# Neighbourhood attention: normalising the outputs instead of the weights, with value tiles in idle weight buffers

## The chip, the core and the metric

The kernel runs on one core of one Trainium2 chip, as one program. The metric is device time in microseconds: the median of the runs of the kernel before is 2946.88 us (three runs, 2945.25 to 2947.84). PE is the matrix engine, with PEld its weight loads; DVE is VectorE, ACT ScalarE, POOL GpSimd, and SP the engine that only issues DMAs here.

## The reference, cut to what matters

The reference is a transformer block (differential attention beside neighbourhood attention, a mixture of experts, a gated embedding) and two layers of retention and stick-breaking attention. The change lies in the neighbourhood attention: 16 heads of 32 columns over 1024 tokens, seen as a grid of 16 rows and 64 columns. A query looks at 8 rows of keys and, within a block of 32 key columns, at 16 of them; the other columns are masked by the bias.

```python
qb = q_row.reshape(b, ncb, Q_COLS, h, d)            # 4 blocks of 16 query columns
kg = k[:, idx].reshape(b, ncb, kr * K_COLS, h, d)   # 8 rows x 32 columns of keys
vg = v[:, idx].reshape(b, ncb, kr * K_COLS, h, d)
sc = jnp.einsum('bjqhd,bjkhd->bhjqk', qb, kg).astype(jnp.float32) * scale + bias
pr = jax.nn.softmax(sc, axis=-1).astype(vg.dtype)
o = jnp.einsum('bhjqk,bjkhd->bjqhd', pr, vg)
```

The softmax subtracts the row's maximum, exponentiates, and divides by the row's sum. Dividing the weights by the sum before the product with the values, or the product after it, is the same arithmetic.

## The kernel before, in words

The first layer runs `project` (all projections; queries, keys and values go to DRAM), `diff_attention`, `nb_attention` and then the output projection `out_proj`. A planner simulates the program when it is built and orders each engine's instructions by it; each engine then runs its queue strictly in that order, and waits on semaphores. Work of one stage is thus issued inside another where it is ready: loads and splits of a later stage stand in the queues of an earlier one.

`nb_attention` (L453) takes the 16 heads in 4 groups of 4. For a group, the queries of four heads are laid on the diagonal of a block matrix (`qbd`, a high and a low part, L485 on ACT and L486 on POOL), the keys are split into a high and a low part (`kh`, `kl`), and the bias is put together on POOL from DMAs (`edge`, `inner`, L497 and L499). Then come four column blocks (`cb`). In each, eight row pairs of queries give eight tiles of 128 rows (4 heads x 2 grid rows x 16 columns) by 256 or 288 keys:

- three matmuls on PE into a bank `sc` (L522 to L524);
- bias and row maximum in one DVE instruction into `P` (L531);
- in two batches of four tiles: the maxima negated on DVE (L534), four exponentials on ACT that also give the row sums (L536), the reciprocal of four sums on DVE (L538), four normalisations on POOL (L540), four transposes on DVE into `pt` (L542), which turn 32x32 blocks.

When all eight tiles are transposed, 16 fp32 matmuls (L551), one per grid row of keys, add the value products of the whole column block into one bank `po`; the first covers all eight tiles, so it needs all transposes. The values of four heads lie on the diagonal of `vbd`, zeroed once by POOL (`zero`, L439) and loaded by four DMAs on SP per block (L508). There are two such tiles, taken in turn. Four copies, two on ACT and two on DVE (L558, L556), bring `po` to `cat`. `P` has eight buffers, `sc` six banks, `po` two.

The weights of `project` and `out_proj` come in chunks of 256 columns: a raw tile `wraw` (one buffer, `w_raw`, L125) is split by ACT and DVE into `whi` and `wlo` (two buffers each, L113 and L114). `out_proj` (L564) takes chunk 0 for tiles 0 to 3, chunk 1 for tiles 0 to 3, and then tiles 4 to 7 of both. In `diff_attention` the q tiles are loaded by POOL's own DMA queue (L377); `lv` and `lp` are small tiles from which lambda is computed.

Of the kernel before, what the change touches and what calls it, by code (L numbers as in the profile page):

```python
# [7 lines left out]
F32 = mybir.dt.float32  # L8
F32R = mybir.dt.float32r
I32 = mybir.dt.int32  # L10
AF = mybir.ActivationFunctionType
OP = mybir.AluOpType
# [32 lines left out]
class Kernel:  # L45
# [289 lines left out]
    def diff_attention(self, cat):  # L335
        tc, nc, I = self.tc, self.nc, self.I
        lam_init = 0.8 - 0.6 * math.exp(0.0)
        with self.banks(mm=2, tp=2, sp=2), self.pool(name="a2k", bufs=2, side="right") as kp, \
                self.pool(name="a2", bufs=2) as wp, self.pool(name="a2c", bufs=1) as cp:

            lv = cp.tile([128, 4, 64], F32, name="lv")
            for j, n in enumerate(("lam_q1", "lam_k1", "lam_q2", "lam_k2")):
                nc.sync.dma_start(lv[:, j], dap(I[n], 0, [[0, 128], [1, 64]]))
            lp = cp.tile([128, 2, 64], F32, name="lp")
            nc.vector.tensor_mul(lp, lv[:, 0:4:2], lv[:, 1:4:2])
# [24 lines left out]
            for h in range(4):  # L370
# [4 lines left out]
                for qt in range(NT):  # L375
                    qr = kp.tile([128, 2, 2, 128], F32R, name="q", bufs=3)
                    nc.gpsimd.dma_start(qr.rearrange("p m c t -> p (m c t)"), self.q_d[h, qt])  # L377
                    sm = self.small.tile([128, 2], F32, name="dsm")
                    e = []
                    for m in range(2):  # L380
                        s = self.s_ps()
# [15 lines left out]
                    for hf in range(2):  # L397
                        p = self.t_ps()
# [42 lines left out]
    def nb_consts(self, cp):  # L441


        qbd = [[cp.tile([128, 2, 8, 4, 32], F32R, name="qbd%s%d" % (n, hf)) for n in "hl"] for hf in range(2)]
        vbd = [cp.tile([128, 16, 128], F32, name="vbd%d" % j) for j in range(2)]
        for hl in qbd:
            for t in hl:
                self.zero(t.rearrange("p c r h q -> p (c r h q)"), 2048)
        for t in vbd:
            self.zero(t.rearrange("p r d -> p (r d)"), 2048)  # L450
        return qbd, vbd

    def nb_attention(self, ep, cat, qbd, vbd):  # L453
# [6 lines left out]
        with self.banks(sc=6, po=2), self.pool(name="a3", bufs=2) as wp, self.pool(name="a3c", bufs=1) as cp:  # L460
# [4 lines left out]
            for j in range(2):  # L465
                t = cp.tile([128, 3744], F32, name="pt%d" % j)
                for row in (6 * NR + 1, 6 * NR + 13):
                    nc.vector.memset(t[:, row * 32:row * 32 + 32], 0.0)
                pt.append(t)
            rmk = cp.tile([128, 9, 32], F32, name="rmk")  # L470
            nc.sync.dma_start(rmk, I["c_nbmask"][:, 96:].rearrange("p (r k) -> p r k", r=9))
            for g in range(4):
# [31 lines left out]
                for cb in range(4):  # L504
                    vb, pT = vbd[cb % 2], pt[cb % 2]
                    for h in range(4):
# [3 lines left out]
                    qh, ql = (t[:, cb % 2].rearrange("p r h q -> p r (h q)") for t in qbd[cb // 2])  # L510
                    for rp0 in (0, 4):
                        mx = self.small.tile([128, 4], F32, name="nmx")
                        sm = self.small.tile([128, 4], F32, name="nsm")
                        ps4 = []
                        for j in range(4):
                            rp = rp0 + j
# [7 lines left out]
                            nc.tensor.matmul(ps[:, :n], ql[:, rp], khv[kv], start=False, stop=True)  # L524
                            p = wp.tile([128, 288], F32, name="P", bufs=8)[:, :n]
                            if nr == 9:
                                bv = inner[KIND[cb]]
                            else:
# [3 lines left out]
                                                           op1=OP.max, scale=1.0, scalar=-3e38, accum_out=mx[:, j:j + 1])  # L532
                            ps4.append((p, rp, r0, n))
                        nc.vector.tensor_scalar(mx, mx, -1.0, None, op0=OP.mult)  # L534
                        for j, (p, rp, r0, n) in enumerate(ps4):
                            nc.scalar.activation(p, p, AF.Exp, bias=mx[:, j:j + 1], accum_out=sm[:, j:j + 1])  # L536
                        rc = self.small.tile([128, 4], F32, name="nrc")
                        nc.vector.reciprocal(rc, sm)  # L538
                        for j, (p, rp, r0, n) in enumerate(ps4):
                            nc.gpsimd.tensor_scalar(p, p, rc[:, j:j + 1], 1.0, op0=OP.mult, op1=OP.mult)  # L540
                            o = (rp * NR + r0 - 2 * rp + 6) * 32
                            nc.vector.transpose(pT[:, o:o + n], p)  # L542


                    po = self.bank("po")
                    for kr_ in (7, *range(7), *range(8, 16)):
                        have = [rp for rp in range(8) if kr_ == 7 or first(rp * 2) <= kr_ < first(rp * 2 + 1) + 8]
                        a, m = have[0], len(have)
                        o = (a * NR + kr_ - 2 * a + 6) * 32
                        w = pT[:, o:o + m * (NR - 2) * 32].rearrange("p (m x) -> p m x", m=m)[:, :, :32]  # L550
                        nc.tensor.matmul(po[:, a * 32:(a + m) * 32], vb[:, kr_], w, start=kr_ == 7, stop=kr_ == 15)  # L551
                    for j in range(4):
                        o = cat[j][:, 4 + g].rearrange("p (r c) -> p r c", c=64)[:, :, cb * 16:cb * 16 + 16]
                        s = po[:, j * 64:j * 64 + 64].rearrange("p (r q) -> p r q", q=16)
                        if j % 2:
                            nc.vector.tensor_copy(o, s)  # L556
                        else:
                            nc.scalar.activation(o, s, AF.Copy)  # L558

# [987 lines left out]
```

## Time and profile before

| what | value |
| --- | --- |
| median of the runs | 2946.88 us |
| profiled execution, its own time | 2949.21 us |
| its span | 2947.4 us |
| mean granted clock of PE | 0.967 |
| busy share of the span: PE, DVE, ACT, POOL | 92%, 72%, 60%, 24% |
| DMA | 512.92 MB, mean 174 GB/s |

The busy shares are means over the whole span; the neighbourhood attention is only the stretch from about 541 to 711 us of it. In the rows below, a timeline row gives the start, the duration, the engine, the line, the operation with output and inputs, the count of merged instructions, and in brackets the idle time before it with what ended it. The granted clock is 1.00 at 2.4 GHz and 0.50 at 1.2 GHz; a value between is a mean over a stretch.

### The profile page before, as it was taken

The page shows a single profiled execution, that of the slowest core. Times are in us where ns is not written, and L with a number is a line of the kernel's source. Part 1 is how long each engine was busy: PE and PEld are TensorE (multiplying, and loading weights), DVE is VectorE, ACT ScalarE, POOL GpSimd, SP SyncE. Part 2 cuts the span into 40 slices and gives each one's busy share as a digit, 9 for nine tenths or more (in the row PEclk, how much of TensorE's full clock was granted, in tenths as well). Part 3 has the DMA queues.
Part 4 walks back from the last instruction along what each step waited for, and adds up shares of the span by engine and source line. Part 5 has one row for each costly group of instructions (what it writes and reads, how often), then busy time and mean ns, then how long its engine had stood idle before and what let it go on. Part 6 is the DMA issues. An engine that isn't in the chain of part 4 may idle for free. (4 is left out here: it accounts for less than half of the span.)

```text
span 2947.4 us, 49384 instructions
## 1 busy us (share of the span) xinstructions
PE 2710.2 (92%) x17751; PEld 2447.2 (83%) x17751; DVE 2127.2 (72%) x4362; ACT 1760.7 (60%) x3827; POOL 718.0 (24%) x847
## 2 busy tenths in 40 slices
PE   7999889788979999999959799999989899999988
PEld 7998878678968777877749788999889788899888
DVE  6778589676389888999965458899355368898354
ACT  4444467554258878888846357788342367788242
POOL 0343131563001102111024101650123102650132
PEclk9999999889989999999979899999999899999999
DMA  7766432324279989999851333322562342331661
GB/s 237 248 204 204 130 79 69 64 50 141 109 272 328 314 313 355 368 363 367 308 211 70 115 120 96 98 87 75 199 217 73 116 128 88 98 95 65 223 190 72
DMA packets 390010, 512.92 MB, mean 174 GB/s; under 512 B 94948, under 2 KB 236284, under 8 KB 389252
## 3 DMA queue, kind: packets, MB, share of 16 engines
q1 hardware_dynamic: 375364, 480.37, 49.3%
q0 software_dynamic: 14400, 29.38, 3.0%
q8 instruction: 141, 2.31, 0.3%
q14 instruction: 105, 0.86, 0.1%
HBM read 425.71 MB, written 101.97 MB: 179 GB/s over the span
## 5 line engine op out<-in xcount | busy, mean ns | idle before, releaser
L150 PE MATMUL mm<-whi,acth 128*128 128x256 f32 x2816 | 812.0, 288 | 20.5 <-ACT acth L113 5.7
L152 PE MATMUL mm<-whi,actl 128*128 128x256 f32 x2816 | 807.4, 287 | 6.4 <-DVE rsx L100 3.8
L151 PE MATMUL mm<-wlo,acth 128*128 128x256 f32 x2816 | 804.8, 286 | 0.0
L150 PEld LDWEIGHTS mm<-whi,acth 128*128 128x128 f32 x2816 | 543.7, 193 | 31.7 <-ACT acth L113 7.9
L152 PEld LDWEIGHTS mm<-whi,actl 128*128 128x128 f32 x2816 | 542.6, 193 | 11.0 <-DVE rsx L100 4.3
L151 PEld LDWEIGHTS mm<-wlo,acth 128*128 128x128 f32 x2816 | 543.2, 193 | 3.0 <-issue 0.9
L114 DVE TENSOR_TENSOR wlo<-mraw,whi 128x512 fp32r<-128x512 f32 x508 | 316.1, 682 | 46.7 <-ACT whi L113 46.4
L113 ACT ACTIVATE whi<-mraw 128x512 fp32r<-128x512 f32 x508 | 276.1, 628 | 11.5 <-PE mm L879 9.3
L114 DVE TENSOR_TENSOR wlo<-wraw,whi 128x2048 fp32r<-128x2048 f32 (+1 forms) x64 | 145.5, 2278 | 138.9 <-ACT whi L113 129.1
L1198 PE MATMUL mm<-acth,whi 128*128 128x512 f32 x512 | 201.7, 394 | 0.0
L1200 PE MATMUL mm<-acth,wlo 128*128 128x512 f32 x512 | 201.1, 393 | 0.0
L1199 PE MATMUL mm<-actl,whi 128*128 128x512 f32 x512 | 200.5, 392 | 0.0
L113 ACT ACTIVATE whi<-wraw 128x2048 fp32r<-128x2048 f32 (+1 forms) x64 | 117.0, 1833 | 102.0 <-PE mm L152 67.6
L1240 POOL TENSOR_TENSOR cN<-rx,rcos 128x256 f32<-128x256 f32 x64 | 63.4, 990 | 444.2 <-ACT rx L1237 440.4
L114 DVE TENSOR_TENSOR mlo<-mraw,mhi 128x512 fp32r<-128x512 f32 x256 | 160.2, 680 | 2.9 <-ACT mhi L113 1.6
L1373 ACT ACTIVATE sw<-sw 128x128 f32<-128x128 f32 (+2 forms) x192 | 100.8, 528 | 70.5 <-DVE sw L1372 69.5
L113 ACT ACTIVATE mhi<-mraw 128x512 fp32r<-128x512 f32 x256 | 140.6, 631 | 2.9 <-PE mm L879 2.9
L920 POOL DMA_INDIRECT y_d<-ey,sidx x32 | 39.0, 1219 | 373.5 <-ACT ey L919 364.8
L1366 DVE SCALAR_TENSOR_TENSOR sw<-z,sw 128x128 f32<-128x128 f32 (+1 forms) x192 | 103.8, 547 | 30.3 <-ACT sw L1365 29.5
L1386 DVE TENSOR_TENSOR sal<-tp,sah 128x512 fp32r<-128x512 f32 (+1 forms) x192 | 101.8, 546 | 25.4 <-ACT sah L1385 24.8
L1363 ACT ACTIVATE sw<-z 128x128 f32<-128x128 f32 (+1 forms) x192 | 93.3, 491 | 38.2 <-DVE z L1360 38.0
L1200 PEld LDWEIGHTS mm<-acth,wlo 128*128 128x128 f32 x512 | 96.2, 188 | 19.6
(361 smaller groups left out, 6776.0 us busy)
## 6 DMA issues: line engine op xcount, KB each, us to landing
mraw<-in_w_dram SPq DMA_DIRECT2D x191, 1024.0 KB, 9.0
wraw<-in_w_in_dram SPq DMA_DIRECT2D x88, 512.0 KB, 4.8
mw<-in_w_ada_dram SPq DMA_DIRECT2D x32, 768.0 KB, 6.7
wraw<-in_w_out_dram SPq DMA_DIRECT2D x24, 512.0 KB, 5.3
q_d<-qo SPq DMA_DIRECT2D x32, 256.0 KB, 3.2
q<-q_d POOLq DMA_DIRECT2D x32, 256.0 KB, 2.9
h_d<-res SPq DMA_DIRECT2D x16, 512.0 KB, 2.7
sqk<-sq_d SPq DMA_DIRECT2D x32, 256.0 KB, 4.1
```

The source lines that it names most:

```text
L113: nc.scalar.activation(hi, raw, AF.Copy)
L114: nc.vector.tensor_sub(lo, raw, hi.bitcast(F32))
L150: nc.tensor.matmul(ps[:, :n], ah[:, k, sl], wh[:, k, :n], start=k == 0, stop=False)
L151: nc.tensor.matmul(ps[:, :n], ah[:, k, sl], wl[:, k, :n], start=False, stop=False)
L152: nc.tensor.matmul(ps[:, :n], al[:, k, sl], wh[:, k, :n], start=False, stop=k == kt - 1)
L1198: nc.tensor.matmul(ps, wh[:, k, cs], hh[:, k], start=k == 0, stop=False)
L1199: nc.tensor.matmul(ps, wh[:, k, cs], hl[:, k], start=False, stop=False)
L1200: nc.tensor.matmul(ps, wl[:, k, cs], hh[:, k], start=False, stop=k == 7)
L1363: nc.scalar.activation(a, z, AF.Abs)
L1366: nc.vector.scalar_tensor_tensor(a, z, 0.0, a, op0=OP.max, op1=OP.add)
L1373: nc.scalar.activation(a, a, AF.Exp)
L1386: nc.vector.tensor_sub(al[ts], pv, ah[ts].bitcast(F32))
```

## The change

Four value tiles replace two: the third and fourth are one buffer of `whi` and one of `wlo`, used as fp32 while the weights don't need them; all four are zeroed by POOL, and column block `cb` always uses tile `cb`. To make room, `lv` and `lp` live in the raw weight buffer. Tiles go in pairs instead of batches of four; the maxima are negated on ACT; the exponentials are transposed as they are. The eight sums of a column block get one reciprocal; POOL spreads it along a diagonal (`dg`, 128x256), one matmul with a 0/1 matrix (`hd1`) brings every reciprocal to all 32 partitions of its head in the second half of the `po` bank, ACT copies it out (`rb`), and DVE multiplies the outputs by it on their way to `cat`. `P` has six buffers.

```diff
-            lv = cp.tile([128, 4, 64], F32, name="lv")
+            lb = self.w_raw()
+            lv = lb[:, 0:256].rearrange("p (j d) -> p j d", j=4)
...
         vbd = [cp.tile([128, 16, 128], F32, name="vbd%d" % j) for j in range(2)]
+        vbd += [self.W.tile([128, 2048], F32, name="vbd", tag=t, bufs=2).rearrange("p (r d) -> p r d", d=128)
+                for t in ("whi", "wlo")]
...
+            hd1 = cp.tile([128, 4, 32], F32, name="hd1")
+            eye = cp.tile([128, 32], F32, name="eye")
+            nc.vector.memset(hd1, 0.0)
+            for h in range(4):
+                b = slice(h * 32, h * 32 + 32)
+                nc.vector.memset(hd1[b, h], 1.0)
+                nc.scalar.activation(eye[b], self.ident[b, b], AF.Copy)
...
-                    vb, pT = vbd[cb % 2], pt[cb % 2]
+                    vb, pT = vbd[cb], pt[cb % 2]
...
-                    for rp0 in (0, 4):
+                    sm = self.small.tile([128, 8], F32, name="nsm")
+                    for rp0 in range(0, 8, 2):
...
-                            p = wp.tile([128, 288], F32, name="P", bufs=8)[:, :n]
+                            p = wp.tile([128, 288], F32, name="P", bufs=6)[:, :n]
...
-                        nc.vector.tensor_scalar(mx, mx, -1.0, None, op0=OP.mult)
-                        for j, (p, rp, r0, n) in enumerate(ps4):
-                            nc.scalar.activation(p, p, AF.Exp, bias=mx[:, j:j + 1], accum_out=sm[:, j:j + 1])
-                        rc = self.small.tile([128, 4], F32, name="nrc")
-                        nc.vector.reciprocal(rc, sm)
-                        for j, (p, rp, r0, n) in enumerate(ps4):
-                            nc.gpsimd.tensor_scalar(p, p, rc[:, j:j + 1], 1.0, op0=OP.mult, op1=OP.mult)
+                        nc.scalar.activation(mx, mx, AF.Copy, scale=-1.0)
+                        for j, (p, rp, r0, n) in enumerate(ps2):
+                            nc.scalar.activation(p, p, AF.Exp, bias=mx[:, j:j + 1], accum_out=sm[:, rp:rp + 1])
                             o = (rp * NR + r0 - 2 * rp + 6) * 32
                             nc.vector.transpose(pT[:, o:o + n], p)
+                    rc = self.small.tile([128, 8], F32, name="nrc")
+                    nc.vector.reciprocal(rc, sm)
+                    dg = wp.tile([128, 8, 32], F32, name="dg", bufs=1)
+                    nc.gpsimd.tensor_tensor(dg, eye.unsqueeze(1).to_broadcast([128, 8, 32]),
+                                            rc.unsqueeze(2).to_broadcast([128, 8, 32]), op=OP.mult)
...
+                    nc.tensor.matmul(po[:, 256:512], hd1.rearrange("p h q -> p (h q)"), dg.rearrange("p r q -> p (r q)"),
+                                     start=True, stop=True)
+                    rb = wp.tile([128, 256], F32, name="rb", bufs=1)
+                    nc.scalar.activation(rb, po[:, 256:512], AF.Copy)
                     for j in range(4):
                         o = cat[j][:, 4 + g].rearrange("p (r c) -> p r c", c=64)[:, :, cb * 16:cb * 16 + 16]
-                        s = po[:, j * 64:j * 64 + 64].rearrange("p (r q) -> p r q", q=16)
-                        if j % 2:
-                            nc.vector.tensor_copy(o, s)
-                        else:
-                            nc.scalar.activation(o, s, AF.Copy)
+                        nc.vector.tensor_mul(o, po[:, j * 64:j * 64 + 64].rearrange("p (r q) -> p r q", q=16),
+                                             rb[:, j * 64:j * 64 + 64].rearrange("p (r q) -> p r q", q=16))
```

## Rows read from the trace of the kernel before

**Rows 1.** Windows: start:end, length, busy us (instructions) by engine, clock, DMA.
```profile
541.00:712.00 171.00, 138.35 (x923) 132.98 (x924) 125.52 (x492) 95.14 (x321) 117.41 (x176) 0.89 0.35 66
...
541.00:584.00 43.00, 34.66 (x212) 32.83 (x213) 32.38 (x115) 22.96 (x73) 36.78 (x50) 0.84 0.46 78
...
627.00:669.00 42.00, 33.96 (x228) 32.70 (x229) 31.78 (x134) 23.25 (x81) 30.96 (x47) 0.88 0.21 39
669.00:711.00 42.00, 35.27 (x255) 34.28 (x254) 31.00 (x126) 22.49 (x80) 18.58 (x38) 0.96 0.33 72
```

**Rows 2.** Timeline of PE, starts of chains of value products.
```profile
555.13 2.46 PE L551 MATMUL po<-pt,vbd 128*128 128x256 f32 x16 [0.87 <-DVE pt L542]
...
591.53 4.31 PE L551 MATMUL po<-pt,vbd 128*128 128x256 f32 x16 [4.60 <-issue]
...
600.75 4.29 PE L551 MATMUL po<-pt,vbd 128*128 128x256 f32 x32
...
681.58 2.36 PE L551 MATMUL po<-pt,vbd 128*128 128x256 f32 x16
...
688.86 1.37 PE L551 MATMUL po<-pt,vbd 128*128 128x256 f32 x9
...
702.16 4.36 PE L551 MATMUL po<-pt,vbd 128*128 128x256 f32 x32 [2.39 <-issue]
```

**Rows 3.** Timeline of POOL around 590 us.
```profile
582.46 6.18 POOL L486 TENSOR_TENSOR qbdl<-qT,qbdh 32x512 fp32r<-32x512 f32 x4
...
589.82 3.78 POOL L540 TENSOR_SCALAR P<-P,nrc 128x288 f32<-128x288 f32 x8
```

**Rows 4.** Groups by line, 541 to 712: count | busy, mean ns | idle before, releasers.
```profile
L536 ACT ACTIVATE P<-P,nmx 128x256 f32<-128x256 f32 (+1 forms) x128 | 65.1, 510 | 56.1 <-DVE nmx L534 55.2 <-DVE cat L556 0.8
L540 POOL TENSOR_SCALAR P<-P,nrc 128x256 f32<-128x256 f32 (+1 forms) x128 | 61.7, 503 | 35.9 <-DVE nrc L538 29.2 <-DVE nmx L534 6.3
L542 DVE STREAM_TRANSPOSE pt<-P 128x256 f32<-128x256 f32 (+1 forms) x128 | 56.4, 451 | 12.4 <-POOL P L540 12.2
...
L486 POOL TENSOR_TENSOR qbdl<-qT,qbdh 32x512 fp32r<-32x512 f32 x24 | 31.4, 1307 | 5.4 <-ACT qbdh L485 4.0
...
L531 DVE CUSTOM_DVE_ANT_0 P<-sc,inner 128x288 f32<-128x288 f32 x64 | 26.8, 432 | 2.6 <-PE sc L524 2.3
...
L534 DVE TENSOR_SCALAR nmx<-nmx 128x4 f32<-128x4 f32 x32 | 12.9, 404 | 0.3
...
L499 POOL TENSOR_TENSOR inner<-edge,rmk 128x288 f32<-128x288 f32 x12 | 9.6, 805 | 0.3
L556 DVE COPY cat<-po 128x64 f32<-128x64 f32 x32 | 7.0, 217 | 8.9 <-ACT cat L558 8.9
...
L538 DVE RECIPROCAL nrc<-nsm 128x4 f32<-128x4 f32 x32 | 5.3, 167 | 16.7 <-ACT P L536 16.5
```

**Rows 5.** Timeline of ACT, two small operations of the projection.
```profile
352.21 0.21 ACT L102 ACTIVATE rsy<-rsx 128x8 f32<-128x8 f32 x1
...
356.27 0.47 ACT L330 ACTIVATE bo<-tp,gbk 128x256 f32<-128x256 f32 x1 [3.61 <-PE tp L321]
```

**Rows 6.** Line 534, durations min/median/max in ns.
```profile
L534 DVE TENSOR_SCALAR nmx<-nmx x32: 127/170/2710, 546.5 to 697.8; 128x4 f32<-128x4 f32 x32
```

**Rows 7.** Timeline of SP, reload of a value tile.
```profile
679.78 1.55 SPq L508 DMA_DIRECT2D vbd<-vb_d  x3
```

**Rows 8.** Timelines of DVE and PE, weight split and output projection.
```profile
352.00 2.29 DVE L114 TENSOR_TENSOR wlo<-wraw,whi 128x2048 fp32r<-128x2048 f32 x1 [1.17 <-ACT whi L113]
...
710.32 6.89 DVE L114 TENSOR_TENSOR actl<-cat,acth 128x1024 fp32r<-128x1024 f32 x6
...
721.18 0.39 PE L150 MATMUL mm<-whi,acth 128*128 128x256 f32 x1 [0.70 <-DVE res L601]
```

**Rows 9.** Timelines of POOL and PE, zeroing and the fourth q load.
```profile
367.06 5.05 POOL L439 TENSOR_SCALAR vbd<-one 128x1024 f32<-128x1024 f32 x4
...
375.98 2.09 PE L385 MATMUL sp<-ks,q 128*128 128x512 f32 x8 [0.53 <-DMA q<-q_d]
```

More of the change, by code (lines that the diff above doesn't have):

```diff
@@ L339, in diff_attention @@
                 self.pool(name="a2", bufs=2) as wp, self.pool(name="a2c", bufs=1) as cp:
-            lv = cp.tile([128, 4, 64], F32, name="lv")
+            lb = self.w_raw()
+            lv = lb[:, 0:256].rearrange("p (j d) -> p j d", j=4)
             for j, n in enumerate(("lam_q1", "lam_k1", "lam_q2", "lam_k2")):
                 nc.sync.dma_start(lv[:, j], dap(I[n], 0, [[0, 128], [1, 64]]))
-            lp = cp.tile([128, 2, 64], F32, name="lp")
+            lp = lb[:, 256:384].rearrange("p (j d) -> p j d", j=2)
             nc.vector.tensor_mul(lp, lv[:, 0:4:2], lv[:, 1:4:2])
@@ L510, in nb_attention @@
                     qh, ql = (t[:, cb % 2].rearrange("p r h q -> p r (h q)") for t in qbd[cb // 2])
-                    for rp0 in (0, 4):
[L512 to L515, printed above, removed]
+                    sm = self.small.tile([128, 8], F32, name="nsm")
+                    for rp0 in range(0, 8, 2):
+                        mx = self.small.tile([128, 2], F32, name="nmx")
+                        ps2 = []
+                        for j in range(2):
                             rp = rp0 + j
@@ L532, in nb_attention @@
                                                            op1=OP.max, scale=1.0, scalar=-3e38, accum_out=mx[:, j:j + 1])
-                            ps4.append((p, rp, r0, n))
-                        nc.vector.tensor_scalar(mx, mx, -1.0, None, op0=OP.mult)
-                        for j, (p, rp, r0, n) in enumerate(ps4):
-                            nc.scalar.activation(p, p, AF.Exp, bias=mx[:, j:j + 1], accum_out=sm[:, j:j + 1])
-                        rc = self.small.tile([128, 4], F32, name="nrc")
-                        nc.vector.reciprocal(rc, sm)
-                        for j, (p, rp, r0, n) in enumerate(ps4):
-                            nc.gpsimd.tensor_scalar(p, p, rc[:, j:j + 1], 1.0, op0=OP.mult, op1=OP.mult)
+                            ps2.append((p, rp, r0, n))
+                        nc.scalar.activation(mx, mx, AF.Copy, scale=-1.0)
+                        for j, (p, rp, r0, n) in enumerate(ps2):
+                            nc.scalar.activation(p, p, AF.Exp, bias=mx[:, j:j + 1], accum_out=sm[:, rp:rp + 1])
                             o = (rp * NR + r0 - 2 * rp + 6) * 32
                             nc.vector.transpose(pT[:, o:o + n], p)
+                    rc = self.small.tile([128, 8], F32, name="nrc")
[3 more added lines that the diff above has]
+                                            rc.unsqueeze(2).to_broadcast([128, 8, 32]), op=OP.mult)
                     po = self.bank("po")
```

## The prediction

> **What bounds the kernel now.** I first looked at the windows of the stretch in which the changed lines run, 541 to 711 us: in 171 us PE is busy 138, DVE 126, POOL 117, ACT 95, and PE's granted clock is 0.84 in the first group, 0.88 in the third, 0.96 in the last [rows 1]. No engine is full. The stage is 16 column blocks (4 groups x 4 values of cb), each ending in one chain of value products, po. So I read PE's timeline for the starts of po: first 555.13, the thirteenth (group 3 begins) 681.58, last 702.16 [rows 2]. Twelve intervals take 126.45 us, 10.54 each; the last three 20.58, 6.86 each. The same work per block at two paces: that difference is what to explain.
>
> In the fast part PE is the limit: between 681.58 and 688.86 (7.28 us) it waits for nothing. In the slow part po is seen to wait, 4.60 us before 591.53 [rows 2]. POOL's timeline says why: it runs the low parts of the next group (L486) for 6.18 us from 582.46, and only from 589.82 the eight normalisations (L540, 3.78 us) whose results the transposes of this block need [rows 3]. POOL's load per block of groups 0 to 2: L540 is 61.7 / 16 = 3.9 us, L486 and L499 are (31.4 + 9.6) / 13 = 3.2 (what is left of them after 541 lies in about the first 13 blocks) [rows 4]. Work due now queues behind work due a group later. The groups by line show who waits in turn: ACT 55.2 us for the negated maximum, POOL 29.2 for the reciprocal, DVE 12.2 for POOL and 8.9 for ACT's copy out of the same bank [rows 4]. Exponential, reciprocal, normalisation, transpose is a round trip over ACT, DVE, POOL and DVE in batches of four.
>
> **The change part by part.**
>
> *Normalising moves from the weights to the outputs.* 128 L540 leave POOL (61.7 us) and the round trip. Added per block: one product 128x256 on POOL (dg; nearest row L499, 128x288, 0.8 us), one fp32 product on PE, one ACT copy 128x256 out of PSUM (rb; nearest row L330, 0.47 us [rows 5]), four DVE products 128x64 in place of two DVE and two ACT copies; one reciprocal of the two goes. The PE product: po's 32 records (16 matmuls, each recorded twice) go over 2240 columns by the loop's bounds and take 4.36 us [rows 2], so 256 columns take 4.36 x 256 / 2240 = 0.50. A DVE product reads PSUM and writes cat like the copy L556, 217 ns [rows 4]: 0.9 a block for 0.44 today. dg can start when the last exponential is done, while the last transposes and 4.36 us of po still run; that hides the reciprocal, dg and most of what may stand ahead of it on POOL. Without that cover PE stands on the product (a rival below).
>
> *Negation on ACT, pairs for fours.* 32 negations leave DVE (12.9 us), 64 smaller ones come to ACT at 0.21 (L102, 128x8 [rows 5]): 13.4 us. A negation takes 127 ns at least, 170 in the median and 2710 at most [rows 6]: on DVE it sometimes stands still. The Trainium skill (SBUF — State Buffer, "Who interferes with whom") has a rule that would do this: a VectorE instruction in a two-port mode and a GpSimd instruction shut each other out for a whole instruction. By it, 12.9 - 32 x 0.17 = 7.5 us of DVE's stage vanish beyond the work itself; if the long ones are only waits for the maxima, nothing does. The sum needs neither, since DVE is not what limits it. ACT after: 95 + 13.4 + 16 x 0.47 = 116 us, 7.2 a block. P has six buffers for eight, but a pair's way (two reductions 0.9, negation 0.2, two exponentials 1.0, two transposes 0.9 [rows 4, 5]) is 3.0 us, and three pairs at once pass four of them in 4.0 us: fewer buffers don't bind.
>
> *Four value buffers.* A reload waits for the po of two blocks before. But that of block 13 is issued from 679.78 on and done issuing at 681.3, over seven us ahead of its po at 688.86, and no wait of that po is seen [rows 2, 7]. I cost this part at 0; loads queued on SP behind it are for a group ahead. Bounds: from a gain of 2 us to a loss of 1.
>
> *What the weight buffers give up.* Today w_out's first two chunks are split before the stage. Now one whi and one wlo hold values until the last po, so chunk 0 takes chunk 1's place at 352 and chunk 1 is split after the stage. It is due when chunk 0's first four tiles are through, at 721.18 today, where PE waits 0.70 us for the residual anyway; DVE's splits of cat run from 710.32 for 6.89 us, and even behind all of them a split of 2.29 ends at 719.5 [rows 8]. Cost 0 to 2 us; I take 0.5. lam's rows pass through the raw buffer ahead of chunk 0, whose split waits till 352 in any case: 0. Zeroing two more buffers repeats today's row of four instructions, 5.05 us. If it stands ahead of the q load that POOL issues at 372, PE, which today waits 0.53 us for that load, waits up to 5 more; if it runs in POOL's idle time before, 0 [rows 9]. I take 2.
>
> **The new pace.** PE's floor is 7.28 + 0.50 = 7.78. DVE: 125.5 - 12.9 (negations) - 2.6 (half of the reciprocals) - 7.0 (copies) + 64 x 0.22 = 117, 7.3 a block. POOL: 117.4 - 61.7 + 16 x 0.8 = 69. PE comes first, with DVE and ACT close behind, in queues that run in order. The interval 591.53 to 600.75, 9.22 us, ends without a wait of po [rows 2]: a block of the first groups with POOL not in the way and the rest uneven. I take the middle of 7.78 and 9.22, 8.5.
>
> **Sum**, against the profiled execution's 2949.2 us: twelve intervals 12 x (8.5 - 10.54) = -24.5; three at the end +0.5 each, +1.5; the first po earlier, as two trips over POOL go, -3 (0 to -5); behind the last po the product, rb and one DVE product, +1.0, ahead of it a reciprocal and a normalisation less, -1.0; zeroing +2; w_out +0.5. Together -23.5, 2925.7; the median of the runs is 2.3 below the profiled one, so 2923.4.
>
> **Rivals.**
> - *PE at its floor* (0.12). Twelve intervals at 7.78, -33; first po -5; +1.5: 2910. For it: at the end PE goes without a gap already. By the rows the clock is higher where PE waits least (0.96 in the last group). The Trainium skill (TensorE: Matmul & The Clock Gate, "What's actually happening") says that a monitor sets the clock by how busy the array has lately been; by that rule closing the gaps gives the clock back as well, and this case follows. Against: DVE at 7.3 and ACT at 7.2 leave little slack.
> - *The trip still sets the pace* (0.16). ACT's 55.2 us on the maxima are DVE against ACT, without POOL. If only POOL's lumps go, intervals fall from 10.54 to 9.7, -10; with 0 to +4 of the other terms 2937 to 2941, and 2944 if the first po gains nothing.
> - *Slower: the product becomes a gate* (0.12). PE runs in order. If the product stands straight behind po and dg waits on POOL behind the next group's L486 (6.18 us at a stretch), PE stops; rb on ACT then stops the exponentials behind it, and the products on DVE the transposes behind them. A full stop costs reciprocal 0.17, dg 0.8, product 0.5, rb 0.47, DVE 0.9: 2.8 a block, 45 us over 16, so -23.5 + 45: 2968. It decides from 23.5 / 16 = 1.5 us a block on, that is when dg ends 1.5 us after po. Against it: POOL has 49 us less to do, and the next block's scores can stand in between.
> - My forecast, a gain of 12 to 32 us: 0.60 (2914 to 2935 on the runs' scale).
>
> **Range and chances.** 0.2% (5.9 us) is about what a measurement of this kernel can tell from no change. Faster: forecast, floor and half of the third case, 0.80; the same: the other half and mild gates, 0.10; slower: 0.10. For 8 in 10, 2908 to 2941.
>
> **What would show it.** Right: po's starts 8 to 9 us apart in groups 0 to 2; nothing of POOL between exponential and transpose; granted clock over 0.9; POOL near 69 us; the residual still what PE meets first at the output projection. Wrong: PE or ACT waiting for dg or rb over 1 us a block; exponentials still 50 us on maxima; over 4 us on a q load near 376; PE waiting for chunk 1's wlo.

## The result and the profile after

The changed kernel takes 2915.34 us in the median of four runs (2912.77 to 2921.78), against 2946.07 for the kernel before on the same chip: ratio 0.9898, 95% interval 0.9882 to 0.9914. That is faster, and inside the predicted range. The predicted 2923.4 was 8 us too high, and the pace came out as the first rival had it (7.75 us an interval, where it had 7.78). The execution that was profiled took 2921.78, 6.4 above its median; the account below is made against it and the 2949.21 of before.

The windows of the stage, from its first score to the output projection's first product; columns as in [rows 1]:

```profile
539.65:672.20 132.55, 126.66 (x929) 123.72 (x929) 112.70 (x473) 105.22 (x366) 65.50 (x64) 0.98 0.36 64
539.65:583.00 43.35, 42.64 (x300) 41.92 (x301) 39.70 (x162) 36.43 (x124) 30.04 (x30) 0.93 0.56 100
583.00:628.00 45.00, 43.72 (x331) 42.94 (x330) 38.82 (x168) 38.05 (x138) 27.29 (x26) 1.00 0.42 76
```

PE is now busy for 126.66 of 132.55 us, 96%, where it was 138.35 of 171, 81% [rows 1]. Its busy time fell although new products came to it; the granted clock rose from 0.89 to 0.98.

The same view of the twelve intervals alone, before and after:

```profile
555.13:681.58 126.45, 101.94 (x673) 97.92 (x674) 92.17 (x365) 70.95 (x246) 95.06 (x139) 0.88 0.32 56
548.51:641.49 92.98, 91.00 (x686) 89.29 (x685) 81.77 (x350) 79.11 (x274) 58.64 (x56) 1.00 0.46 82
```

PE's idle time there falls from 24.5 us to 2.0, and its busy time by 10.9, at a granted clock of 1.00 in place of 0.88: of the 33.5 us that went, two thirds are waits of PE and one third is busy time, which got shorter at the higher clock although new products came to it.

PE's timeline, starts of po (first, eighth, thirteenth and last of the sixteen):

```profile
548.51 2.36 PE L566 MATMUL po<-pt,vbd 128*128 128x256 f32 x16
...
604.68 2.46 PE L566 MATMUL po<-pt,vbd 128*128 128x256 f32 x16 [1.28 <-DVE pt L550]
...
641.49 2.35 PE L566 MATMUL po<-pt,vbd 128*128 128x256 f32 x16
...
663.14 2.45 PE L566 MATMUL po<-pt,vbd 128*128 128x256 f32 x16
```

Twelve intervals take 641.49 - 548.51 = 92.98 us, 7.75 each, against 10.54 in [rows 2]; the last three 7.22 each, against 6.86. Of sixteen chains only that at 604.68 shows a wait ahead of its start. In the mean the two paces of before have become nearly one; single intervals still range from 6.3 to 9.9 us.

The groups by line in the stage (count | busy, mean ns of one | idle before, releasers):

```profile
L548 ACT ACTIVATE P<-P,nmx 128x256 f32<-128x256 f32 (+1 forms) x128 | 65.6, 513 | 1.5
L550 DVE STREAM_TRANSPOSE pt<-P 128x256 f32<-128x256 f32 (+1 forms) x128 | 54.1, 443 | 8.3 <-ACT P L548 7.7
L498 POOL TENSOR_TENSOR qbdl<-qT,qbdh 32x512 fp32r<-32x512 f32 x24 | 32.3, 1347 | 7.2 <-ACT qbdh L497 5.8
L546 ACT ACTIVATE nmx<-nmx 128x2 f32<-128x2 f32 x64 | 12.3, 196 | 14.3 <-DVE nmx L543 13.9
L567 PE MATMUL po<-dg,hd 128*128 128x256 f32 x32 | 10.2, 402 | 0.0
L556 POOL TENSOR_TENSOR dg<-eye,nrc 128x256 f32<-128x256 f32 x16 | 9.9, 617 | 40.2 <-DVE nrc L554 40.2
L573 DVE TENSOR_TENSOR cat<-po,rb 128x64 f32<-128x64 f32 x64 | 9.7, 212 | 0.0
L570 ACT ACTIVATE rb<-po 128x256 f32<-128x256 f32 x16 | 5.9, 371 | 8.8 <-PE po L567 8.6
```

ACT's wait for the maxima, 56.1 us ahead of the exponentials in [rows 4], is now 1.5 there and 14.3 ahead of the negations. The added operations cost nearly what the nearest rows gave: POOL's product 0.62 (estimated 0.8), rb 0.37 (0.47), the products of the outputs 0.21 (0.22). The product on PE cost less than the 0.50 that was estimated. Its two records overlap with their neighbours, so the step from start to start counts, 553.67 - 553.37 = 0.30 us in the first block, and 0.24 to 0.30 in 14 of the 16:

```profile
553.37 0.65 PE L567 MATMUL po<-dg,hd 128*128 128x256 f32 x2
553.67 0.48 PE L534 MATMUL sc<-kh,qbdh 128*128 128x288 f32 x1
```

PE never waits for dg (0.0 ahead of L567): POOL itself stood idle 40.2 us until the reciprocals came.

The lumps are still on POOL's queue, but nothing of the trip passes them. POOL's timeline:

```profile
582.29 0.62 POOL L556 TENSOR_TENSOR dg<-eye,nrc 128x256 f32<-128x256 f32 x1
582.86 3.96 POOL L498 TENSOR_TENSOR qbdl<-qT,qbdh 32x512 fp32r<-32x512 f32 x3
...
590.23 0.62 POOL L556 TENSOR_TENSOR dg<-eye,nrc 128x256 f32<-128x256 f32 x1
```

**Where the 27.4 us of the two profiled executions come from.** Each line is the difference between starts that both traces show; the last one reaches to the time of the execution:

| stretch | before | after | difference |
| --- | --- | --- | --- |
| to the first score | 541.1 | 539.6 | -1.4 |
| first score to first po | 14.1 | 8.9 | -5.2 |
| twelve intervals | 126.45 | 92.98 | -33.5 |
| last three intervals | 20.6 | 21.7 | +1.1 |
| last po to the experts' first transpose | 150.1 | 155.9 | +5.7 |
| the experts | 626.9 | 624.1 | -2.8 |
| last expert product to the next layer's first transposed product (L1198 before), the gated embedding between them | 197.6 | 204.3 | +6.7 |
| all behind it | 1272.4 | 1274.4 | +2.0 |

Up to the last po 39.0 us were gained, 37.6 of them in the stage, more than I said; 5.7 went right behind it, and the 2100 us from the experts on, which the change doesn't touch, lost 5.9 more.

**The 5.7 us behind the last po.** Timelines of DVE, SP and PE after:

```profile
668.51 2.29 DVE L114 TENSOR_TENSOR wlo<-wraw,whi 128x2048 fp32r<-128x2048 f32 x1 [1.72 <-PE po L566]
...
670.90 0.48 DVE L573 TENSOR_TENSOR cat<-po,rb 128x64 f32<-128x64 f32 x3
...
687.49 1.42 DVE L617 TENSOR_TENSOR res<-mm,res 128x256 f32<-128x256 f32 x4 [6.16 <-DMA res<-in_x_dram]
```
```profile
670.87 0.95 SPq L122 DMA_DIRECT2D wraw<-in_w_out_dram  x2
672.12 0.37 SPq L609 DMA_DIRECT2D res<-in_x_dram  x1
```
```profile
672.18 0.58 PE L150 MATMUL mm<-whi,acth 128*128 128x256 f32 x1 [3.22 <-ACT acth L113]
```

The split of the second weight chunk stands on DVE ahead of the last products with rb, of which the first starts at 670.77 and the row shows the other three; PE waits 3.22 us for the output projection, against 1.40 before. The same split frees the raw weight buffer, so the load of the third chunk now stands on SP at 670.87 right ahead of the residual's. In the kernel before the third chunk came at 354 and the residual was issued 4.4 us after the last po began, not 9.0:

```profile
354.32 0.94 SPq L122 DMA_DIRECT2D wraw<-in_w_out_dram  x2
...
706.55 0.38 SPq L593 DMA_DIRECT2D res<-in_x_dram  x1
```

The first sum with the residual comes 15.3 us behind the first product of the projection (687.49 - 672.18), against 720.7 - 707.9 = 12.8.

**Zeroing.** POOL's timeline has the two tiles that it now zeroes before the q loads in one stretch of idle time, and PE's timeline the q load that [rows 9] has:

```profile
326.16 4.10 POOL L440 TENSOR_SCALAR vbd<-one 128x1024 f32<-128x1024 f32 x4 [39.96 <-PE mm L151]
```
```profile
377.87 2.12 PE L386 MATMUL sp<-ks,q 128*128 128x512 f32 x8 [0.42 <-DMA q<-q_d]
```

The wait is 0.42 us, against 0.53 before.

### The profile page after: what moved, and what is told of

The parts are those of the page before. It is cut to its first block, busy times and chain, and to the rows that moved or that the text cites. A ratio compares the mean times of both kernels' runs of the same rounds, so it can differ in the third digit from the quotient of the medians.

```text
span 2919.7 us, 49355 instructions
## 1 busy us (share of the span) xinstructions
PE 2709.7 (93%) x17783; PEld 2449.4 (84%) x17783; DVE 2118.4 (73%) x4351; ACT 1772.3 (61%) x3879; POOL 669.0 (23%) x739
## 4 chain that ended last, share of the span: by engine, by line
PE 51%; DVE 18%; issue 12%; DMA 8%; ACT 8%; POOL 2%; SPq 1%; DVEq 0%; ACTq 0%; POOLq 0%
PE mm L152 6%; PE mm L150 6%; PE mm L151 6%; PE mm L1214 3%; PE mm L1215 3%; PE mm L1216 3%; DVE sw L1383 3%; PE mm L893 3%; PE mm L895 3%; PE mm L894 3%; PE po L566 2%; DVE wlo L114 2%; DMA sqk<-sk_d 2%; PE mm L406 2%; PE sp L386 2%
```

## The experiments

Every kernel was timed beside the kernel before on its own chip, so ratios are compared. The stretches are those of the one profiled execution of each kernel, which lies up to 6.4 us from its median. "Interval" is (start of the thirteenth po minus start of the first) / 12; "stage" reaches from the first score to the start of the last record of po (165.1 us before, 128.6 after); "end" from there to the experts' first transpose; "embedding" from the last expert product to the first transposed product (L1198 before) of the layer behind the gated embedding; the gated embedding itself lies within that stretch.

| kernel | ratio to before, 95% | interval | stage | end | embedding |
| --- | --- | --- | --- | --- | --- |
| before | 1 | 10.54 | 165.1 | 146.1 | 197.6 |
| after | 0.9898, 0.9882 to 0.9914 | 7.75 | 128.6 | 150.8 | 204.3 |
| e1_two_values | 0.9889, 0.9874 to 0.9903 | 7.88 | 129.2 | 146.4 | 202.9 |
| e2_four_values_only | 1.0005, 0.9995 to 1.0016 | 10.57 | 167.2 | 145.9 | 204.5 |
| e7_no_low_parts | 0.9953, 0.9937 to 0.9969 | 8.82 | 144.5 | 145.3 | 201.8 |
| e5_pool_pairs | 0.9982, 0.9973 to 0.9992 | 10.16 | 158.4 | 145.9 | 200.7 |
| e10_pool_load2 | 0.9937, 0.9923 to 0.9952 | 8.65 | 141.3 | 154.5 | 191.9 |
| e6_fours | 0.9924, 0.9906 to 0.9942 | 9.21 | 143.9 | 147.7 | 201.6 |
| e3_neg_on_dve | 0.9885, 0.9866 to 0.9904 | 8.21 | 134.1 | 150.9 | 192.1 |
| e4_neg_on_act_only | 0.9959, 0.9944 to 0.9973 | 9.68 | 153.9 | 146.7 | 200.7 |
| e11_neg_by_reduce | 0.9993, 0.9982 to 1.0004 | 10.25 | 161.7 | 146.4 | 198.6 |
| e12_pairs_neg_by_reduce | 0.9869, 0.9849 to 0.9889 | 8.00 | 131.0 | 150.4 | 195.0 |
| e8_turn_rb | 0.9847, 0.9828 to 0.9865 | 7.69 | 125.8 | 148.1 | 192.9 |
| e9_turn_rb_two_values | 0.9878, 0.9861 to 0.9895 | 7.87 | 127.4 | 146.7 | 196.6 |

### What are four value tiles worth? (e1_two_values, e2_four_values_only)

e1 is the kernel after with two value tiles, and lam's rows in their own tiles again; e2 makes the opposite edit in the kernel before. Of e1's edit:

```diff
-        vbd += [self.W.tile([128, 2048], F32, name="vbd", tag=t, bufs=2).rearrange("p (r d) -> p r d", d=128)
-                for t in ("whi", "wlo")]
...
-                    vb, pT = vbd[cb], pt[cb % 2]
+                    vb, pT = vbd[cb % 2], pt[cb % 2]
```

> The changed kernel with two value tiles again, both weight buffers left to w_out, and lam's rows in their own tile. Theory (the gain is the normalisation leaving POOL and the round trip; the reload of a value tile is never what po waits for): the first twelve intervals between po's starts stay at 7.7 to 7.9 us, the time stays within 3 us of the changed kernel, perhaps 1 to 2 us shorter because chunk 1 of w_out is split before the stage again: 2912 to 2918. Rival (SP's 59 us of waiting for po were part of the slow pace, so four tiles carry a part of the gain): intervals of 8.3 or more, 2924 or more.

> The kernel before with the four value tiles alone. Theory: nothing is gained, intervals stay near 10.5, 2943 to 2949 (0 to +3 for the later split of chunk 1). Rival: a gain of 8 us or more, 2938 or less.

e1 took 2915.7 us and e2 2951.1: neither differs from its base by what can be measured. Four tiles bring nothing in either kernel. In the kernel after they also cost: with the weight buffers left alone, the end is 146.4 us in place of 150.8, so of the 5.7 us the 4.7 that the end lost go with the buffers that are lent out (the rest lies in the last po itself). Lending alone doesn't cost this: e2 and e5 lend the same buffers, their split stands behind the last po too, and their end is 145.9. There a first copy of po runs on ACT beside the split, and the residual's load is issued ahead of the third chunk's (707.07 and 709.43 in e2). So the rows put the price on the lending together with outputs that are all multiplied on DVE behind the split, and with the order on SP; the shares of these two were not separated. In e1's total the saving doesn't show beyond the scatter.

### Lumps on POOL's queue, or the trip itself? (e7_no_low_parts, e5_pool_pairs, e10_pool_load2)

e7 is the kernel before without the low parts of the queries in groups 1 to 3, so these groups use the low parts of group 0. e5 is the kernel after with the weights normalised on POOL again, in pairs. e10 is e1 with POOL's load put back, but as products that only need the row sum and whose output nobody uses. (The first form, e10_pool_load, gave this output a tile of its own; the pool then needs 32.5 kb a partition where 31.9 are left, so there is no time for it.)

```diff
# e7
-                        nc.gpsimd.tensor_tensor(lo, s, hi.bitcast(F32), op=OP.subtract)
+                        if g == 0:
+                            nc.gpsimd.tensor_tensor(lo, s, hi.bitcast(F32), op=OP.subtract)
# e5 (and no dg, product, rb; outputs copied as before)
+                        rc = self.small.tile([128, 2], F32, name="nrc")
+                        nc.vector.reciprocal(rc, sm[:, rp0:rp0 + 2])
+                        for j, (p, rp, r0, n) in enumerate(ps2):
+                            nc.gpsimd.tensor_scalar(p, p, rc[:, j:j + 1], 1.0, op0=OP.mult, op1=OP.mult)
# e10
                             nc.vector.transpose(pT[:, o:o + n], p)
+                            nc.gpsimd.tensor_scalar(scr[:, :n], rmk.rearrange("p r k -> p (r k)")[:, :n],
+                                                    sm[:, rp:rp + 1], 1.0, op0=OP.mult, op1=OP.mult)
```

> The kernel before without the low parts of the queries in groups 1 to 3 (the instructions of POOL that make them are left out, so those scores use group 0's low parts): POOL loses 31 us of lumps up to 6.2 us, the normalisation stays on POOL. Theory (work due a group later stands in POOL's queue ahead of work due now): the first twelve intervals fall from 10.5 to 8.5 or less, 2920 to 2930. Rival (the round trip over four engines itself sets the pace, lumps or not): intervals of 9.8 or more, 2938 or more.

> The changed kernel with the weights normalised on POOL again, in pairs, with the copies of po as before; four value tiles, pairs and the negation on ACT stay. Theory (normalising on a POOL queue that is also filled with the next group's work is what slowed it): intervals of 9.5 to 10.5, PE seen waiting for transposes and DVE for POOL, 2935 to 2948. Rival (batches of four and DVE's negation made the round trip long, pairs shorten it, POOL may stay in it): intervals of 8.5 or less, 2925 or less.

> The kernel after with two value tiles (as e1_two_values, 2915.7), and POOL given 128 extra products of 128x256 or 128x288, at the places where the kernel before normalised the weights, with an operand that is ready only after the exponential; their output is used by nobody. So POOL's load is as before the change, but nobody waits for these products except dg, which stands behind them in POOL's queue. Theory (about 21 of the 33 us came from the lumps on POOL's queue, the rest from the trip by itself): intervals 8.2 to 9.2, as dg is late behind the lumps, 2922 to 2932. Rival A: POOL's load by itself slows the stage (its port to the SBUF shared with DVE, or its queue): intervals of 10 or more, 2938 or more. Rival B: only the weights' trip over POOL counts: intervals under 8, 2912 to 2918.

e7: 2935.86 us, 8.82 an interval, between the two expectations: without the lumps 20.7 of the 33.5 us of the intervals go, with the trip still on POOL. e5: 2943.68, 10.16, as expected. With pairs, ACT's negation and four value tiles in place, the intervals are nearly as long as before as long as weights pass POOL. e5's waits in the stage (line, what was waited for: us, times, longest):

```profile
PE sc L527 <- DVE nmx L536: 19.2, 9, 4.6
DVE pt L547 <- POOL P L545: 16.4, 19, 2.9
```

PE stands at the scores, since DVE, whose transposes stand behind POOL, reaches the reductions late. e10: 2930.0, 8.65, as the theory had it. POOL does its old work, in lumps like this of nine products, and only dg is behind them, for which PE waits twice, 3.7 us in all:

```profile
621.16 0.62 POOL L556 TENSOR_TENSOR dg<-eye,nrc 128x256 f32<-128x256 f32 x1
621.76 5.19 POOL L549 TENSOR_SCALAR scr<-rmk,nsm 128x288 f32<-128x288 f32 x9
626.91 1.26 POOL L496 TENSOR_TENSOR qbdl<-qT,qbdh 32x512 fp32r<-32x512 f32 x1
```

That load costs 12 x (8.65 - 7.88) = 9 us in the intervals, and from e5 to e10, where the load stays and only the trip leaves POOL, 12 x (10.16 - 8.65) = 18. So, taken away in this order, the trip over POOL is the larger part and the length of its queue the smaller. The parts don't add up independently: e7 shortens the queue first and gets 20.7 us by that, since the lumps cost most where the trip stands behind them. (e10's end of 154.5 is its own: its unused output sat in a weight buffer, whose split waited 6.2 us for it.)

### Pairs for fours (e6_fours)

e1 with batches of four; `P` has eight buffers again, and dg and rb lie in the freed weight buffer.

```diff
-                    for rp0 in range(0, 8, 2):
+                    for rp0 in (0, 4):
...
-                            p = wp.tile([128, 288], F32, name="P", bufs=6)[:, :n]
+                            p = wp.tile([128, 288], F32, name="P", bufs=8)[:, :n]
```

> The changed kernel with two value tiles, in batches of four with eight buffers of P (dg and rb in the weight buffer that this frees). Theory (it is the trip over POOL that went, not the batch): intervals 7.8 to 8.3, 2914 to 2922, the first po about 1.5 us later. Rival (pairs are what lets PE run through): intervals of 9 or more, 2928 or more.

2926.07 us, 9.21 an interval: my expectation of 7.8 to 8.3 missed. Batches of four cost 12 x (9.21 - 7.88) = 16 us. In these intervals PE is idle for 11.4 us (3.3 in e1) and busy for 99.2 (91.2), at a granted clock of 0.94 (1.00 in e1). PE's timeline of e6 shows a part of the waits, and DVE's what ends the first one: the fifth and sixth of the eight transposes.

```profile
579.76 4.63 PE L564 MATMUL po<-pt,vbd 128*128 128x256 f32 x16 [2.84 <-DVE pt L548]
...
616.38 4.12 PE L564 MATMUL po<-pt,vbd 128*128 128x256 f32 x16 [2.81 <-DVE pt L548]
```
```profile
578.88 0.82 DVE L548 STREAM_TRANSPOSE pt<-P 128x288 f32<-128x288 f32 x2
```

They end at 579.70, and the last two transposes run from 579.99 to 581.13, when po has begun. So, other than was said of the kernel before, po's start doesn't need all eight: its first product reads, in place of the last two tiles, two rows of `pt` that were set to zero.

With POOL in the trip smaller batches show no such gain. e4 below, with batches of four and ACT's negation, has intervals of 9.68; e5, with pairs, six buffers of `P` and four value tiles, has 10.16. Whether the pairs or the fewer buffers make e5 the slower one was not separated.

### The negation: place, or long instructions? (e3, e4, e11, e12)

e4 makes one edit in the kernel before, the negation on ACT. e3 takes it back in the kernel after, to DVE. e11 (in the kernel before) and e12 (in the kernel after) do it on DVE by a reduction over one element.

```diff
# e4 in the kernel before (e3 is the reverse in the kernel after)
-                        nc.vector.tensor_scalar(mx, mx, -1.0, None, op0=OP.mult)
+                        nc.scalar.activation(mx, mx, AF.Copy, scale=-1.0)
# e11, e12
+                        mn = self.small.tile([128, 4], F32, name="nmn")
+                        nc.vector.tensor_reduce(mn, mx.unsqueeze(2), axis=AX.X, op=OP.max, negate=True)
```

> The changed kernel with the maxima negated on DVE again, in pairs. Theory: DVE gets 64 instructions of 0.13 to 0.17, 10 us, and ACT loses 12; DVE goes from 6.7 to 7.4 us a block, still under PE's 7.78, and POOL has little left that could hold the negation up, so its mean is under 0.25 us: intervals 7.7 to 8.2, 2915 to 2922. Rival (the negation on DVE, held up behind POOL and queued behind transposes, was a good part of the slow pace): intervals of 8.6 or more, 2926 or more.

> The kernel before with one edit: the negation of the row maxima, in batches of four, on ACT in place of DVE. Theory: the exponentials' 55 us of idle time ahead of them is time in which ACT has nothing due, since the trip over POOL sets the pace; moving the negation gains nothing on that path but a hop: intervals 10.3 to 10.6, 2943 to 2950. Rival: the hop from DVE's negation to ACT, and DVE's long negations (up to 2.71 us), are part of the pace: intervals 9.9 or less, 2939 or less.

> The kernel before with one edit: the negation of the row maxima stays on DVE, in batches of four, but is done by a reduction over one element with its sign turned, in place of the product with -1. e4_neg_on_act_only gained about 10 us (2939.1 against 2949.0) by moving the negation to ACT. In the kernel before, the long negations end where an instruction of POOL ends (574.60 + 2.71 = 577.31, POOL's L497 from 576.12 for 1.16 ends at 577.28). Theory: the product with -1 is a form that DVE can't run beside POOL's instruction, and the exponentials stand behind it; the reduction is a form that can: no negation over 0.3 us, intervals 9.6 to 10.0, 2936 to 2943. Rival 1 (the hop and DVE's queue): ACT gains because the negation no longer goes through DVE; then the reduction on DVE gives intervals of 10.3 or more, 2945 or more, though it is short. Rival 2: the reduction stands still as the product does: durations up to 2 us, nothing gained.

> The kernel after with the same reduction on DVE, in pairs, in place of ACT's negation. With the product with -1 on DVE (e3_neg_on_dve) the intervals were 8.2 and the stage 134.1 us from the first score to the last value product, against 7.75 and 128.6 with the negation on ACT. Theory (the stalls of the product make the difference): no negation over 0.3 us, intervals 7.7 to 7.9, stage 127 to 130. Rival (DVE's queue is full enough that 64 more instructions hold up the transposes): intervals 8.1 or more, stage 132 or more, though no negation is long. In all: 2903 to 2917, the width from the stretch after the experts, which the stage doesn't touch and which has been 192 to 204 us long so far.

e4 took 2939.14 us with 9.68 an interval: my theory, no gain, fell, and the rival was right. Moving 32 instructions of 0.2 us brought 10 us. Why? In the kernel before, the longest negation and what POOL did meanwhile (DVE's timeline, then POOL's):

```profile
574.60 2.71 DVE L534 TENSOR_SCALAR nmx<-nmx 128x4 f32<-128x4 f32 x1
```
```profile
575.36 0.82 POOL L499 TENSOR_TENSOR inner<-edge,rmk 128x288 f32<-128x288 f32 x1
576.12 1.16 POOL L497 TENSOR_TENSOR edge<-edge,msk 128x448 f32<-128x448 f32 x1
```

It ends at 577.31, and POOL's second instruction at 577.28. All ten negations over 0.25 us end 0.02 to 0.04 us after an instruction of POOL, and so do all 22 of e3. The Trainium skill (SBUF — State Buffer, "Who interferes with whom") says that a tensor_scalar on DVE, as this product is, can run in a two-port mode, that it and an instruction of POOL then shut each other out for a whole instruction, and that a reduction never contends; the rows agree, 32 of 32 long negations ending with POOL's, and e11 shows the second half. The negation's line in e11 (min/median/max in ns):

```profile
L535 DVE TENSOR_REDUCE nmn<-nmx x32: 111/152/158, 548.7 to 696.6; 128x4 f32<-128x4 f32 x32
```

No reduction is over 158 ns, and the line's busy time fell from 12.9 us [rows 4] to 4.6. But e11 gained only 12 x (10.54 - 10.25) = 3.5 us in the intervals and nothing that can be measured in all (2948.03). All engines of e11 run the order of the kernel before, instruction by instruction, so this is what the long instructions cost. The first rival was right, but for its bound of 10.3: e4's gain is mostly the place. On ACT the negation leaves DVE's queue, and the planner writes another order of the scores and reductions around it; which of the two makes the 12 x (10.25 - 9.68) = 7 us stays open.

e3's 8.21 and 2914.37 lie at the edge of what I expected, and not for my reason: its negations took 0.36 us in the mean (23.0 / 64), not under 0.25. In the kernel after, the same pair: with the product on DVE the stage is 134.1 us (e3), with the reduction, in the same order, 131.0 (e12), with ACT 128.6. e12's 8.00 lies between what theory and rival had: about half is the long instructions, half the place. In all e3 (2914.37) and e12 (2911.86) are no slower than after; their embedding is 9 to 12 us shorter.

### Without the product (e8_turn_rb, e9_turn_rb_two_values)

POOL spreads the reciprocals over 32 columns, and one DVE transpose turns them into rb; the product on PE and ACT's copy go. e9 has two value tiles besides.

```diff
-            nc.vector.memset(hd1, 0.0)
...
+            nc.vector.memset(eye, 1.0)
...
+                    rb = wp.tile([128, 256], F32, name="rb", bufs=1)
+                    nc.vector.transpose(rb, dg.rearrange("p r q -> p (r q)"))
...
-                    nc.tensor.matmul(po[:, 256:512], hd1.rearrange("p h q -> p (h q)"), dg.rearrange("p r q -> p (r q)"),
-                                     start=True, stop=True)
-                    rb = wp.tile([128, 256], F32, name="rb", bufs=1)
-                    nc.scalar.activation(rb, po[:, 256:512], AF.Copy)
```

> The changed kernel without the product on PE and the copy on ACT: POOL spreads the reciprocals over 32 columns, and one DVE transpose 128x256 (some 0.42 us) turns them into rb. Theory (PE is at its floor, so what leaves PE is gained): intervals fall by up to 0.5 to 7.3 to 7.5, and behind the last po about 1 us goes: 4 to 9 us less than the changed kernel, 2906 to 2912. Rival (DVE, 7.1 us a block with it, is the limit as well): intervals 7.7 or more, 2914 to 2920.

> The kernel after with the product replaced by a transpose on DVE (as in e8_turn_rb) and with two value tiles and the weight buffers left alone (as in e1_two_values). Theory: both edits stand side by side and neither binds: intervals 7.6 to 7.9 in the first twelve blocks, stage (first score to the start of the last po) 125 to 128 us, against 128.6 in after; no wait for the second chunk's split. Of the stretch between the last expert product and the gated embedding, which the stage does not touch, I expect one of the two lengths seen so far: 192 to 193, then 2900 to 2908 in all, or 202 to 204, then 2910 to 2917. Rival: four value tiles are needed once the pace is higher: po waits for values, intervals over 8.2, 2915 or more.

e8 took 2904.39 us, the lowest median of all: its interval of ratios (0.9828 to 0.9865) lies below that of the kernel after. But the pace that I expected, 7.3 to 7.5, did not come: it is 7.69, next to the rival's 7.7. e8's twelve intervals:

```profile
551.36:643.65 92.29, 87.66 (x671) 86.21 (x670) 86.93 (x365) 78.25 (x270) 59.06 (x56) 1.00 0.47 83
```

PE is busy for 3.3 us less than in the kernel after and idle for 2.6 more (4.6 against 2.0), with DVE at 86.93 in place of 81.77. What left PE mostly became waiting. The added line of e8 and the start of its output projection:

```profile
L554 DVE STREAM_TRANSPOSE rb<-dg 128x256 f32<-128x256 f32 x16 | 6.7, 418 | 1.3 <-POOL dg L551 1.3
```
```profile
669.78 0.38 PE L150 MATMUL mm<-whi,acth 128*128 128x256 f32 x1 [1.47 <-ACT acth L113]
```

The transpose takes 0.42 us where PE's product (0.30 from start to start) and ACT's copy (0.37) stood, and rb no longer waits for po: PE's wait at the end is 1.47 in place of 3.22. But of the 15.4 us by which e8's profiled execution is shorter than that of after, the stage gives 2.8 and the end 2.7; 11.4 are the embedding, which no edit touches. e9 is the check: stage 127.4 as expected by the same measure (the expectation names the start of the last po, its 128.6 of after is to the last record), no wait for the split, and an embedding of 196.6, a third length where I expected one of two. Its 2912.47 is no better than the kernel after. So e8 is the better kernel as it stands; by itself its edit is worth 2.8 + 2.7 = 5.5 us beside the kernel after, and with two value tiles (e9 beside e1) 1.8 - 0.3 = 1.5.

### The embedding's 192 to 204 us

The same lines take 191.9 to 204.5 us there in fourteen kernels, and windows from about 37 us behind the last expert product show PE busy for longer in one kernel than in another. After, then e8:

```profile
1480.00:1500.00 20.00, 10.39 (x57) 9.45 (x58) 18.05 (x31) 10.21 (x22) 2.73 (x2) 0.63 0.60 210
1500.00:1520.00 20.00, 16.67 (x139) 16.24 (x138) 14.97 (x30) 7.43 (x19) 6.86 (x5) 0.96 0.30 102
```
```profile
1478.00:1498.00 20.00, 13.64 (x82) 12.64 (x83) 16.26 (x29) 10.30 (x23) 1.79 (x2) 0.69 0.64 211
1498.00:1518.00 20.00, 19.59 (x166) 19.35 (x165) 16.05 (x35) 12.39 (x36) 9.54 (x10) 1.00 0.30 106
```

POOL's order there is the same in after and e8. PE, DVE, ACT and SP have other orders (PE runs part of its transposes at other places between the same products), since the planner orders the whole program anew for each kernel. e11 and before, and e12 and e3, share all orders, and there the lengths differ by 1.0 and 2.9 us; across orders by up to 12.6. That the orders make this difference was not tested by an edit of its own.

## Why the prediction was right, and where its steps were not

- **What bounds the kernel** (two paces; work due now queues behind work due a group later): right. e7 takes the lumps away and the intervals fall by 1.7 us; e5 leaves the trip on POOL and they hardly fall. One reading under it was loose: the wait of 4.60 us before 591.53 has no releaser in its row, and of the eight normalisations from 589.82 only the first four are of that block. DVE's timeline of before has the link: the fifth and sixth transposes wait for POOL and end at 591.32, 0.2 us ahead of po.

```profile
590.36 0.96 DVE L542 STREAM_TRANSPOSE pt<-P 128x288 f32<-128x288 f32 x2 [0.60 <-POOL P L540]
```

- **The new pace, 8.5**: mis-sized. Measured 7.75, so the term of -24.5 is -33.5. I took the middle between PE's floor, 7.78, and an interval of the old kernel, and gave the floor alone 0.12, because DVE and ACT at 7.3 and 7.2 leave little slack. PE came to its floor all the same, with a clock of 0.98 for 0.89 in the stage. The Trainium skill (TensorE: Matmul & The Clock Gate, "What's actually happening") lets the clock follow how busy the array has been; the rows agree, 0.89 with PE busy for 81% of the time, 0.98 with 96%. That the figure of 7.78 was hit to 0.03 is luck: PE's busy time is 91.00 / 12 = 7.58 an interval, that is 7.28 and 0.30 for the product (not 0.50), and 0.17 of waiting makes up the rest. That the slack is small was right: without the product on PE, e8 stays at 7.69. ACT's 7.2 left out that 32 copies, 6.8 us, go from it: 109 us in the stage by the same sum, not 116; the window after has 105.22.
- **Pairs and negation, costed at nothing**: wrong as steps, and part of the same term. I argued that DVE does not limit, so where the negation stands makes no odds. It stands in the trip, and there e4 gains 10 us by it and e6 loses 16 without pairs. Engine totals said nothing on it; the 55 us of ACT's wait for nmx did, and I had the row. With POOL still in the trip, though, pairs showed no gain (e5 beside e4).
- **First po, -3**: -5.2, just past my bound of -5.
- **Four value buffers, 0**: right (e1, e2).
- **The weight buffers, 0.5, and the end, 0**: mis-sized. I followed the split to its due time, but not what its late end releases: the products behind it on DVE (PE's wait 3.22 for 1.40) and the third chunk's load on SP ahead of the residual. Measured +4.7, which e1 gives back; in e2 and e5, where ACT copies part of po, the same loan costs nothing. Nor is the residual what PE meets first at the output projection: before it was ACT's split of cat (1.40 us), and after it is that again (3.22).
- **Zeroing, +2**: 0, the other bound; POOL did it in idle time.
- **The product as a gate**: did not happen; dg has POOL idle ahead of it.
- **Not foreseen**: 5.9 us lost further on, most of it in the embedding. It takes back a part of what the mis-sized pace gave, so the total is closer to the forecast than its terms are, and that is luck: by the experts' start 33.3 us were gained where the sum had 23.5.

## What to carry to other kernels

Where one block of work takes two paces in the same stage, the fast one is the floor to plan for once the cause of the slow one is gone. The engines' totals don't price a round trip over engines with ordered queues: here one hop less was worth 10 us (e4), and smaller batches were worth 16 us once POOL was out of the trip (e6), but showed no gain with POOL in it (e5 beside e4). A buffer lent out may be paid for at its return: follow what the late split holds up and releases, on the DMA queue too. A change of one stage in a planned program moves stages that it doesn't touch by several microseconds, so compare stretches before totals.

## What was not expected of the hardware

- A DVE product on 128x4 elements took 2.71 us beside POOL's instructions, a reduction of the same elements never over 0.158 us. All 32 long products of two kernels end 0.02 to 0.04 us after an instruction of POOL. The whole of it was worth 3.5 us to the stage.
- One DVE transpose of 128x256 (0.42 us) spreads a reciprocal per row over 32 partitions as a PE product (0.30 from start to start) and an ACT copy (0.37) did.
